# Attention scores: ScalarE casts half of the first two units, and the transposes of k or q of a unit share one PSUM tile of 8 KB per partition

## Chip, cores, metric

One core of one Trainium2 chip, one launch. The metric is device time in microseconds (us). Time before: 202.47 us, median of 3 runs (202.41 to 202.62).

## The reference

Scores of attention without softmax, for 8 batches x 8 heads x 512 positions x 64 dimensions, all in float32:

```python
def reference(q, k):
    scale = 1.0 / np.sqrt(q.shape[-1])
    return (np.einsum('bhqd,bhkd->bhqk', q, k) * scale).astype(np.float32)
```

It reads 16.78 MB and writes 67.11 MB, whatever the kernel does between.

## The kernel before

It works in four units of two batches. Per unit it loads k and q in float32 (4.19 MB), casts them to bf16, transposes them on TensorE through PSUM, copies the result to SBUF, and then makes four output tiles of 4.19 MB. An output tile takes eight evacuations, turn by turn on ScalarE and VectorE, and leaves with one store. Inputs and outputs share one pool of three buffers of 32 KB per partition. The copies of the next unit's transposes are put between the evacuations of the present unit by a generator, `ahead`. All DMAs are issued by SyncE (SP), on one queue.

```python
    W = 8                      # transposes per PSUM tile; JP = 16 per unit for k, 16 for q
    big_pool = ctx.enter_context(tc.tile_pool(name="big", bufs=3))
    tpsum_pool = ctx.enter_context(tc.tile_pool(name="tpsum", bufs=2, space=bass.MemoryType.PSUM))
    psum_pool = ctx.enter_context(tc.tile_pool(name="psum", bufs=2, space=bass.MemoryType.PSUM))
    # ... cut ...
    def load_and_cast(v):
        xf = big_pool.tile([P, 2, 2, J * D], f32, name="big")
        both = []
        for x, src in enumerate((k_r, q_r)):
            nc.sync.dma_start(out=xf[:, x], in_=src[v].rearrange("p (s c) -> p s c", s=2))
        for x in range(2):
            xb = bf_pool.tile([P, JP, 2, D, 2], bf16, name="xb")
            wide = (1, RO)[x]
            for s in range(2):
                pinned(nc.gpsimd.tensor_copy(out=..., in_=...))      # 128x2048
            both.append(words(xb.rearrange("p j s d e -> p j (s d e)")))
        return both

    def rearrange(tp, pattern, dst):
        nonlocal n_tp
        copy = (nc.vector.tensor_copy, nc.scalar.copy)[n_tp % 2]
        n_tp += 1
        for s in range(2):                       # two halves of the partitions
            src = tp[half(s)].rearrange(pattern, n=N, h=2)
            for h in range(2):
                pinned(copy(out=dst(s, h), in_=src[:, h]))
                yield
    # transpose(v, kb, qb): W transposes into one tp, then rearrange(tp), for k and then for q

    def scores(v, t):
        kT, qz = ts[v]
        o = big_pool.tile([P, 2, RO, S], f32, name="big")
        for x in range(2):
            n = 2 * t + x
            for i in range(0, RO, 2):
                ps = psum_pool.tile([P, 2, S], f32, name="ps")
                # ... two matmuls into ps ...
                evacuate(o[:, x, i:i + 2, :], ps)
                yield
        nc.sync.dma_start(out=out_r[v, t], in_=o.rearrange("p x i k -> p x (i k)"))
    # ... cut ...
    cast = [load_and_cast(v) for v in range(UNITS)]
    for _ in transpose(0, *cast[0]):
        pass
    for v in range(UNITS):
        ahead = transpose(v + 1, *cast[v + 1]) if v + 1 < UNITS else iter(())
        for t in range(TILES):
            for n, _ in enumerate(scores(v, t)):
                take(ahead, 1 if v == 0 else int(n in (0, 2, 3, 5, 6)))
```

`pinned` keeps each engine's order of work as the program has it; the framework adds the waits.

Of the kernel before, what the change touches and what calls it, by code (L numbers as in the profile page):

```python
# [1 line left out]

# [5 lines left out]


@with_exitstack  # L10
def kernel(
    ctx: ExitStack,
    tc: tile.TileContext,
    q: bass.AP,
    k: bass.AP,
    out: bass.AP,
):







    nc = tc.nc
    B, H, S, D = q.shape
    scale = 1.0 / (D ** 0.5)
    P = 128
    UNITS = B // 2
    N = H  # L30
    M = P // (2 * H)
    R = S // M
    J = R // 2
    RO = 8
    U = S // RO
    JP = J // 2
    JJ = J // RO // 2
    W = 8
    IW = W // JJ
    TILES = N // 2  # L40

    f32 = mybir.dt.float32
    bf16 = mybir.dt.bfloat16

    q_r = q.rearrange("(v b) g (m j) d -> v (b g m) (j d)", b=2, j=R)
    k_r = k.rearrange("(v b) g (m j) d -> v (b g m) (j d)", b=2, j=R)
    out_r = out.rearrange("(v b) (t x h) (u i) k -> v (b t) (h u) x (i k)", b=2, x=2, h=2, i=RO)

    consts = ctx.enter_context(tc.tile_pool(name="consts", bufs=1))

    big_pool = ctx.enter_context(tc.tile_pool(name="big", bufs=3))
    bf_pool = ctx.enter_context(tc.tile_pool(name="bf", bufs=6))
    t_pool = ctx.enter_context(tc.tile_pool(name="t", bufs=2))
    tpsum_pool = ctx.enter_context(tc.tile_pool(name="tpsum", bufs=2, space=bass.MemoryType.PSUM))
    psum_pool = ctx.enter_context(tc.tile_pool(name="psum", bufs=2, space=bass.MemoryType.PSUM))


    pinned = tc.keep_in_program_order

    n_evac = 0  # L60
    n_tp = 0

    def evacuate(dst, src):
        nonlocal n_evac
        if n_evac % 2 == 0:
            pinned(nc.scalar.mul(out=dst, in_=src, mul=scale))  # L66
        else:
            pinned(nc.vector.tensor_scalar(out=dst, in0=src, scalar1=scale, scalar2=None,  # L68
                                           op0=mybir.AluOpType.mult))
        n_evac += 1  # L70

    def half(h):
        return slice(h * D, (h + 1) * D)

    def words(ap):
        return ap.bitcast(f32)

    def load_and_cast(v):

        xf = big_pool.tile([P, 2, 2, J * D], f32, name="big")  # L80
        both = []
        for x, src in enumerate((k_r, q_r)):
            nc.sync.dma_start(out=xf[:, x], in_=src[v].rearrange("p (s c) -> p s c", s=2))
        for x in range(2):
            xb = bf_pool.tile([P, JP, 2, D, 2], bf16, name="xb")

            wide = (1, RO)[x]
            for s in range(2):
                pinned(nc.gpsimd.tensor_copy(  # L89
                    out=xb[:, :, s].rearrange("p (g i) d e -> p g e i d", i=wide),  # L90
                    in_=xf[:, x, s].rearrange("p (g e i d) -> p g e i d", e=2, i=wide, d=D)))
            both.append(words(xb.rearrange("p j s d e -> p j (s d e)")))
        return both

    def rearrange(tp, pattern, dst):

        nonlocal n_tp
        copy = (nc.vector.tensor_copy, nc.scalar.copy)[n_tp % 2]
        n_tp += 1
        for s in range(2):  # L100
            src = tp[half(s)].rearrange(pattern, n=N, h=2)
            for h in range(2):
                pinned(copy(out=dst(s, h), in_=src[:, h]))  # L103
                yield

    def transpose(v, kb, qb):


        kT = t_pool.tile([P, N, M, 2, J], bf16, name="kT")
        qz = qzs[v % 2]  # L110
        ts[v] = (kT, qz)
        kw = words(kT)
        qw = words(qz)
        for j0 in range(0, JP, W):
            tp = tpsum_pool.tile([P, W, P], f32, name="tp")
            for j in range(W):
                pinned(nc.tensor.transpose(out=tp[:, j, :], identity=identity, in_=kb[:, j0 + j]))  # L117
            yield
            yield from rearrange(tp, "d j (n h m) -> d h n m j",
                                 lambda s, h: kw[half(h), :, :, s, j0:j0 + W])  # L120
        for i0 in range(0, RO, IW):
            tp = tpsum_pool.tile([P, IW, JJ, P], f32, name="tp")
            for i in range(IW):
                for jj in range(JJ):
                    pinned(nc.tensor.transpose(out=tp[:, i, jj, :], identity=identity,  # L125
                                               in_=qb[:, RO * jj + i0 + i]))
            yield
            yield from rearrange(tp, "d i jj (n h m) -> d h i n m jj",
                                 lambda s, h: qw[half(h), i0:i0 + IW, :, h * U // 2:(h + 1) * U // 2]
                                 .rearrange("d i n (m s jj) -> d s i n m jj", s=2, jj=JJ)[:, s])  # L130
# [9 lines that stand above are left out]
                for w in range(2):  # L140
                    pinned(nc.tensor.matmul(out=ps[:, w, :], lhsT=qz[:, i + w, n, :],  # L141
                                            rhs=kT[:, n].rearrange("d m s j -> d (m s j)"),
                                            start=True, stop=True))
# [4 lines that stand above are left out]
    def take(steps, count):  # L148
        for _ in range(count):
            next(steps, None)  # L150

    identity = consts.tile([P, P], dtype=f32)
    make_identity(nc, identity)
    qzs = [consts.tile([P, RO, N, P], bf16, name=f"qz{n}") for n in range(2)]
    for qz in qzs:
        nc.vector.memset(qz, 0.0)  # L156
    cast = [load_and_cast(v) for v in range(UNITS)]

    ts = {}
    for _ in transpose(0, *cast[0]):  # L160
        pass
    for v in range(UNITS):
        ahead = transpose(v + 1, *cast[v + 1]) if v + 1 < UNITS else iter(())
        for t in range(TILES):
            for n, _ in enumerate(scores(v, t)):

                take(ahead, 1 if v == 0 else int(n in (0, 2, 3, 5, 6)))
        for _ in ahead:
            pass


# [1 line left out]
_INS = ['q', 'k']  # L173
_OUTS = [((8, 8, 512, 512), 'float32')]


# [23 lines left out]
```

## Time and profile before

| | before |
|---|---|
| time, span | 202.47 us, 200.7 us |
| DMA queue busy | 98.3% of the span |
| busiest compute engines | VectorE 53%, TensorE 52%, ScalarE 42% |
| first store issued; loads through | 36.81 us; about 41.7 us |
| smallest time from issue to landing of a store | 16.0 us |

The prediction below shows the lines. Read it with one thing in mind: when the DMA queue is full from 4 us to the end (a share of 1.01 and 430 GB/s from 4 to 190 us), an engine matters only through the moment at which its work lets the next DMA be issued.

Two more stretches of the kernel before serve for comparison later, the passage from loads to stores and the stores (length, busy time of PE, PEld, VectorE, ScalarE and GpSimd, granted clock, DMA share, GB/s):

```profile
41.00:44.00 3.00, 1.78 (x6) 0.57 (x6) 2.96 (x4) 1.64 (x3) 2.74 (x2) 1.00 0.93 393
44.00:190.00 146.00, 85.10 (x298) 32.80 (x297) 82.56 (x76) 69.19 (x77) 4.04 (x2) 0.82 1.01 430
```

### The profile page before, as it was taken

The numbers are of one execution on the slowest core, as the hardware profiler recorded it, in microseconds if no ns is written. First come the engines' busy times: TensorE is split into PE (matmuls) and PEld (weight loads), VectorE is DVE, ScalarE is ACT, GpSimd is POOL, SyncE is SP. The second block draws the span as 40 slices with busy tenths as digits, with TensorE's granted clock in tenths as the row PEclk, the third lists the DMA queues.
The fourth block names the chain that finished last, engine by engine and source line by source line (L and its number), as shares of the span: only waits on it lengthen the run. The fifth ranks groups of instructions, "written<-read, shape, count | busy, mean of one in ns | idle before, by whom it ended". The sixth has DMA issues, their size and how long they took to land.

```text
span 200.7 us, 1143 instructions
## 1 busy us (share of the span) xinstructions
PE 105.3 (52%) x384; PEld 45.8 (23%) x384; DVE 106.8 (53%) x98; ACT 85.0 (42%) x97; POOL 39.5 (20%) x22
## 2 busy tenths in 40 slices
PE   0035758566657465478637496748585667510000
PEld 0034535223214131224313122312121111100000
DVE  6705538486475976485749357844444444630000
ACT  2004423864755629253844384366435243620000
POOL 1299999995000000000000000000000000000000
PEclk9999576999699999957999759975858858975555
DMA  6999999999999999999999999999999999999994
GB/s 206 424 444 437 421 421 441 434 395 421 434 424 441 428 431 431 433 426 434 431 428 424 434 441 424 431 431 434 424 431 434 431 424 431 428 437 428 428 428 199
DMA packets 5509, 83.95 MB, mean 418 GB/s; under 512 B 384, under 2 KB 384, under 8 KB 384
## 3 DMA queue, kind: packets, MB, share of 16 engines
q1 hardware_dynamic: 5504, 83.89, 98.3%
q8 instruction: 3, 0.05, 0.1%
q14 instruction: 2, 0.02, 0.0%
HBM read 16.78 MB, written 67.11 MB: 418 GB/s over the span
## 4 chain that ended last, share of the span: by engine, by line
DMA 40%; DVE 10%; PE 8%; ACT 6%; issue 1%; ACTq 0%; SPq 0%; DVEq 0%
DMA out_dram<-big 40%; DVE big L68 9%; PE ps L141 8%; ACT big L66 5%; ACT qz L103 1%; DVE qz L103 1%; ACTq L66 0%; SPq L146 0%; DVEq L68 0%
## 5 line engine op out<-in xcount | busy, mean ns | idle before, releaser
L141 PE MATMUL ps<-kT,qz 128*128 128x512 bf16 x256 | 87.6, 447 | 55.5 <-ACT big L66 41.6
L68 DVE TENSOR_SCALAR big<-ps 128x1024 f32<-128x1024 f32 x64 | 78.4, 1224 | 59.8 <-PE ps L141 37.2
L66 ACT ACTIVATE big<-ps 128x1024 f32<-128x1024 f32 x64 | 65.5, 1023 | 73.0 <-PE ps L141 37.2
L141 PEld LDWEIGHTS <-qz 128*128 128x128 bf16 x256 | 27.2, 106 | 111.0 <-issue 97.5
L89 POOL CAST xb<-big 128x2048 bf16<-128x2048 f32 x16 | 38.8, 2468 | 7.9 <-DMA big<-in_k_dram 7.3
L117 PE MATMUL tp<-identity,xb 128*128 128x128 f32 x64 | 11.6, 346 | 13.4 <-POOL xb L89 13.4
L103 ACT COPY kT<-tp 64x512 f32<-64x512 f32 x16 | 9.2, 577 | 15.3 <-PE tp L117 15.1
L103 DVE COPY kT<-tp 64x512 f32<-64x512 f32 x16 | 11.0, 686 | 6.3 <-PE tp L117 6.0
L117 PEld LDWEIGHTS tp<-identity,xb 128*128 128x128 f32 x64 | 10.5, 184 | 15.2 <-POOL xb L89 13.4
L103 DVE COPY qz<-tp 64x512 f32<-64x512 f32 x16 | 11.0, 687 | 2.7 <-PE tp L125 2.5
L103 ACT COPY qz<-tp 64x512 f32<-64x512 f32 x16 | 9.6, 602 | 2.9 <-PE tp L125 2.7
L125 PE MATMUL tp<-identity,xb 128*128 128x128 f32 x64 | 9.4, 300 | 2.5 <-ACT kT L103 2.5
L125 PEld LDWEIGHTS tp<-identity,xb 128*128 128x128 f32 x64 | 8.5, 156 | 4.3 <-issue 3.3
L156 DVE MEMSET qz<- 128x4096 uint32 x2 | 6.9, 3472 | 2.5 <-PEq L184 1.7
L103 ACT ACT_TABLE_LOAD x1 | 1.3, 1283 | 0.7 <-PEq L184 0.7
masks.py:199 POOL TENSOR_SCALAR_AFFINE_SELECT identity<-identity 128x128 f32<-128x128 f32 x1 | 0.3, 292 | 0.1
masks.py:197 POOL MEMSET identity<- 128x128 f32 x1 | 0.2, 204 | 0.3 <-POOLq L184 0.3
L184 POOL MEMSET const-float32-0.0<- 128x1 f32 x1 | 0.1, 98 | 0.2 <-issue 0.2
L184 POOL MEMSET const-bfloat16-1.0<- 128x1 bf16 x1 | 0.1, 101 | 0.0
L184 POOL MEMSET const-uint8-127<- 128x1 uint8 x1 | 0.1, 101 | 0.0
L184 POOL MEMSET const-float32-1.0<- 128x1 f32 x1 | 0.1, 98 | 0.0
## 6 DMA issues: line engine op xcount, KB each, us to landing
out_dram<-big SPq DMA_DIRECT2D x16, 4096.0 KB, 20.7
big<-in_k_dram SPq DMA_DIRECT2D x4, 2048.0 KB, 18.1
big<-in_q_dram SPq DMA_DIRECT2D x4, 2048.0 KB, 22.7
```

The source lines that it names most:

```text
L66: pinned(nc.scalar.mul(out=dst, in_=src, mul=scale))
L68: pinned(nc.vector.tensor_scalar(out=dst, in0=src, scalar1=scale, scalar2=None, op0=mybir.AluOpType.mult))
L89: pinned(nc.gpsimd.tensor_copy(out=xb[:, :, s].rearrange("p (g i) d e -> p g e i d", i=wide), in_=xf[:, x, s].rearrange("p (g e i d) -> p ...
L103: pinned(copy(out=dst(s, h), in_=src[:, h]))
L117: pinned(nc.tensor.transpose(out=tp[:, j, :], identity=identity, in_=kb[:, j0 + j]))
L125: pinned(nc.tensor.transpose(out=tp[:, i, jj, :], identity=identity, in_=qb[:, RO * jj + i0 + i]))
L141: pinned(nc.tensor.matmul(out=ps[:, w, :], lhsT=qz[:, i + w, n, :], rhs=kT[:, n].rearrange("d m s j -> d (m s j)"), start=True, stop=True))
L156: nc.vector.memset(qz, 0.0)
L184: nc = _bacc.Bacc("TRN2", target_bir_lowering=False, num_devices=1)
```

## The change

The intent is to start sooner and to copy in larger pieces: ScalarE takes half of the casts of units 0 and 1, so that a load is cast in half the time; 16 transposes go into one PSUM tile of 8 KB per partition (16 x 128 float32; before, two tiles of half that), which leaves in four wide copies instead of eight; and for unit 0, whose copies nothing else covers, the two engines take turns at these copies.

```diff
-    W = 8
+    W = 16
-    tpsum_pool = ctx.enter_context(tc.tile_pool(name="tpsum", bufs=2, space=bass.MemoryType.PSUM))
+    tpsum_pool = ctx.enter_context(tc.tile_pool(name="tpsum", bufs=1, space=bass.MemoryType.PSUM))
@@ load_and_cast(v) becomes load(v), which issues the two loads, and cast(v, xf)
-                pinned(nc.gpsimd.tensor_copy(
+                to_bf16 = nc.scalar.copy if s and v < 2 else nc.gpsimd.tensor_copy
+                pinned(to_bf16(
@@ rearrange
-        copy = (nc.vector.tensor_copy, nc.scalar.copy)[n_tp % 2]
+        copies = (nc.vector.tensor_copy, nc.scalar.copy)
+        first = len(ts) == 1
         n_tp += 1
-                pinned(copy(out=dst(s, h), in_=src[:, h]))
+                pinned(copies[(n_tp + h * first) % 2](out=dst(s, h), in_=src[:, h]))
@@ body
-    cast = [load_and_cast(v) for v in range(UNITS)]
+    xfs = [load(v) for v in range(3)]
     ts = {}
-    for _ in transpose(0, *cast[0]):
+    for _ in transpose(0, *cast(0, xfs[0])):
         pass
+    xfs.append(load(3))
+    casts = [None] + [cast(v, xfs[v]) for v in range(1, UNITS)]
-                take(ahead, 1 if v == 0 else int(n in (0, 2, 3, 5, 6)))
+                take(ahead, int(n in ((1, 3, 6), (1, 4))[t % 2]))
```

More of the change, by code (lines that the diff above doesn't have):

```diff
@@ L76, in words, with load, cast @@
         return ap.bitcast(f32)
-    def load_and_cast(v):
+    def load(v):
         xf = big_pool.tile([P, 2, 2, J * D], f32, name="big")
-        both = []
         for x, src in enumerate((k_r, q_r)):
             nc.sync.dma_start(out=xf[:, x], in_=src[v].rearrange("p (s c) -> p s c", s=2))
+        return xf
+    def cast(v, xf):
+        both = []
         for x in range(2):
@@ L156 @@
         nc.vector.memset(qz, 0.0)
-    cast = [load_and_cast(v) for v in range(UNITS)]
+    xfs = [load(v) for v in range(3)]
     ts = {}
-    for _ in transpose(0, *cast[0]):
+    for _ in transpose(0, *cast(0, xfs[0])):
         pass
+    xfs.append(load(3))
+    casts = [None] + [cast(v, xfs[v]) for v in range(1, UNITS)]
     for v in range(UNITS):
-        ahead = transpose(v + 1, *cast[v + 1]) if v + 1 < UNITS else iter(())
+        ahead = transpose(v + 1, *casts[v + 1]) if v + 1 < UNITS else iter(())
         for t in range(TILES):
             for n, _ in enumerate(scores(v, t)):
-                take(ahead, 1 if v == 0 else int(n in (0, 2, 3, 5, 6)))
+                take(ahead, int(n in ((1, 3, 6), (1, 4))[t % 2]))
         for _ in ahead:
```

## The prediction

> **What bounds the kernel now.** I read the page first, then windows of the DMA share, then the waits of the DMA queue, then the order of time in the first 60 us, because the change works mostly there.
>
> The page, DMA queue and traffic (packets, MB, share of the span of 16 engines):
>
> ```profile
> q1 hardware_dynamic: 5504, 83.89, 98.3%
> HBM read 16.78 MB, written 67.11 MB: 418 GB/s over the span
> ```
>
> Every byte crosses one queue, and that queue is busy for 98.3% of the span. No compute engine passes 53%. The stretches (columns: length, busy PE, PEld, DVE, ACT, POOL, clock, DMA share, GB/s) show where the other 1.7% lies:
>
> ```profile
> 0.00:2.00 2.00, 0.00 (x0) 0.00 (x0) 0.34 (x1) 1.26 (x1) 0.70 (x6) 1.00 0.42 82
> 2.00:4.00 2.00, 0.00 (x0) 0.00 (x0) 2.00 (x1) 0.02 (x1) 0.00 (x0) 1.00 0.65 221
> 4.00:31.00 27.00, 10.96 (x49) 8.26 (x50) 12.94 (x14) 6.83 (x10) 22.20 (x10) 0.87 1.01 433
> 41.00:43.00 2.00, 1.20 (x5) 0.40 (x5) 1.99 (x3) 1.25 (x2) 1.92 (x1) 1.00 0.89 369
> 4.00:190.00 186.00, 105.29 (x384) 45.83 (x384) 104.45 (x98) 83.73 (x96) 38.80 (x16) 0.83 1.01 430
> ```
>
> A ramp in the first 4 us moves 2 x 82 + 2 x 221 = 606 KB; then it is flat at 430 GB/s. The rest, 83.28 MB at 430 GB/s, takes 193.7 us, so the stream ends near 198 us, and some 2.5 us of tail give the span of 200.7. The time reported, 202.47, is 1.8 us above the span. The only dip is at 41 to 43 us: 2 us x (430 - 369) / 430 = 0.3 us. It lies where the loads end and the stores begin: summing the stretches, the 16.78 MB of loads are through at about 41.7 us.
>
> So the question for any change is: **does each store stand in the queue before the queue runs dry?** A store has 4.19 MB, 9.75 us at 430 GB/s. The stores by line (count, ns, first and last start; then issue to landing):
>
> ```profile
> L146 SPq DMA_DIRECT2D out_dram<-big x16: 372/372/403, 36.8 to 178.1; - x16
> DMA to landing us min/median/max: 16.0/20.7/22.0
> ```
>
> 9.75 us of transfer and about 2 us of completion (the tail again, an estimate) leave at least 16.0 - 11.8 = 4.3 us of standing in the queue for the tightest store, and 20.7 - 11.8 = 9 us for the median one. The queue is therefore never short of work. The issues at the start are at 36.81, 47.49, 56.55 and 64.24 us; they are needed at 41.7, 51.7, 61.4 and 71.2 (one transfer after another). The slacks are 4.9, 4.2, 4.9 and 7.0 us. These are what the change may spend for nothing, or gain for nothing.
>
> The opening, in order of time (start, length):
>
> ```profile
> 8.58 34.34 POOL L89 CAST xb<-big 128x2048 bf16<-128x2048 f32 x14 [7.28 <-DMA big<-in_k_dram]
> 13.44 3.68 PE L117 MATMUL tp<-identity,xb 128*128 128x128 f32 x16 [13.44 <-POOL xb L89]
> 19.61 2.57 PE L125 MATMUL tp<-identity,xb 128*128 128x128 f32 x16 [2.49 <-ACT kT L103]
> 23.57 1.03 PE L141 MATMUL ps<-kT,qz 128*128 128x512 bf16 x2 [1.40 <-DVE qz L103]
> 28.13 1.02 ACT L66 ACTIVATE big<-ps 128x1024 f32<-128x1024 f32 x1 [3.42 <-POOL xb L89]
> 36.81 0.40 SPq L146 DMA_DIRECT2D out_dram<-big  x1
> ```
>
> GpSimd casts without a pause, and the first output tile waits for it: that tile takes the buffer of unit 1's input, free only when unit 1 is cast. Later tiles wait for a landed store:
>
> ```profile
> SPq L146 <- DVE big L68: 152.5, 16, 17.6
> ACT big L66 <- DMA out_dram<-big: 31.3, 12, 3.5
> DVE big L68 <- DMA out_dram<-big: 15.5, 9, 2.5
> ```
>
> The queue's 152.5 us of waiting for VectorE looks like a bound by VectorE; it isn't, because stores already issued keep running during it.
>
> [...]
>
> **The change part by part.** Rows used (busy us, mean ns):
>
> ```profile
> L68 DVE TENSOR_SCALAR big<-ps 128x1024 f32<-128x1024 f32 x64 | 78.4, 1224 | 59.8 <-PE ps L141 37.2
> L66 ACT ACTIVATE big<-ps 128x1024 f32<-128x1024 f32 x64 | 65.5, 1023 | 73.0 <-PE ps L141 37.2
> L89 POOL CAST xb<-big 128x2048 bf16<-128x2048 f32 x16 | 38.8, 2468 | 7.9 <-DMA big<-in_k_dram 7.3
> L103 ACT COPY kT<-tp 64x512 f32<-64x512 f32 x16 | 9.2, 577 | 15.3 <-PE tp L117 15.1
> L103 DVE COPY kT<-tp 64x512 f32<-64x512 f32 x16 | 11.0, 686 | 6.3 <-PE tp L117 6.0
> ```
>
> *Casts.* Four of GpSimd's 16 casts go to ScalarE. GpSimd loses 4 x 2.47 = 9.9 us. ScalarE gains 4 casts of 2048 elements; from 577 ns at 512 and 1023 at 1024 the slope is 0.87 ns per element, so about 1.9 us each, 7.6 us in all. Beside each other, half a load is cast in 2.5 us instead of 4.9.
>
> *Copies.* 64 copies of 512 elements become 32 of 1024. Taking the evacuations as a measure (1.22 and 1.02 us), a unit's copies cost VectorE 4 x 1.22 = 4.9 us instead of 8 x 0.687 = 5.5, and ScalarE 4.1 instead of 4.7. That saves 0.6 us per unit and engine, 2.4 us per engine in all, none of it on the DMA path.
>
> *Buffers.* The four PSUM banks were two tiles and become one. The transposes of q can no longer run during the copies of k, and sixteen transposes come in one burst (16 x 0.30 to 0.35 = 5 us of TensorE).
>
> *The opening.* Loads land at 8.6, 13.4, then every 4.84 us: 18.3, 23.1, 27.9, 32.8, 37.6, 43. k of unit 0 is cast at 11.1 (was 13.4) and transposed at 14.8 (16 in 3.68 us). ScalarE must first cast its half of q (13.4 to 15.3). Four copies follow. If the two engines exclude each other[...], they take 3.5 us[...] to 4.6 us, ending at 18.9 to 20.0. q is transposed in 2.6 us, 21.5 to 22.6, and copied by 25.0 to 27.2. ScalarE next has unit 1's two casts, in program order before any evacuation: 3.8 us, so the first evacuation starts at 28.8 to 31.0, against 28.13. If the copies did overlap fully, it would be some 2 us before 28.13. The first tile took 36.8 - 28.1 = 8.7 us; with the burst I allow 9.3. **The first store is then issued at about 38.1 to 40.3** (35 if the copies overlap); it is needed at 41.7. The second tile needs the buffer of unit 2, whose halves GpSimd still casts alone: q lands at 32.8, two casts end at 37.7, as good as the 37.95 of before. Its 8 to 9 us end at 47 to 50, needed at 51.7. The third tile waits for unit 3, whose q lands at 43 with or without the change, cast at 48.0; with the burst of q's transposes ahead it ends near 57, needed at 61.4.
>
> *Later.* A tile with a burst takes some 11 us instead of 9, the next one 8, against 9.75 of transfer and 9 us of standing queue. Nothing runs dry.
>
> *Sum:* removed from the DMA path, 0; added, 0 to 1 us at the first store; bytes, rate, ramp and tail unchanged. 202.47 + 0.1 = 202.6 us.
>
> **The rivals.** (1) The earlier casts show at the end: if stores waited for compute in the opening, a start 2 us earlier would give 200.5 us. Against it: the queue still has 4.9 us of loads in it when the first store is issued. (2) The serial copies and the two extra ScalarE casts ahead of the first evacuation make the first store late. [...]the store comes at 42 to 43: the queue runs dry by about 1 us, 203.5. Against it: my worst sum without throttle is still 1.4 us early. (3) The single tile starves later stores: a tile would have to last over 19 us, or several in a row over 9.75; 206 or more. Against it: VectorE's sum is 24.5 us of 39 per unit, TensorE's 105.3 / 4 = 26.
>
> **Range and chances.** The three runs of before span 0.2 us[...]: floor 202.1. Rival 2, at one in five, sets the top: 203.8. Over 2% slower means 206.5, a hole of 4 us in the queue, of which I see no source: 0.02. Over 2% faster means 198.4, less than the stream's 193.7 us with its ramp, tail and the 1.8 us outside: 0.01.
>
> **What would show it right or wrong.** Right: queue share still 98%, 430 GB/s in the middle, first store between 35 and 41 us, ScalarE's casts near 1.9 us, copies near 1.0 and 1.2 us, load of unit 3 issued near 16 us (was 18.3), the shortest store landing still over 12 us. The copies of unit 0 alternating without overlap confirm the exclusion. Wrong: a hole in the DMA row at 41 to 45 us or at any later store, or a rate other than 430 GB/s with the same bytes.

The forecast came to 202.6 us (202.47 + 0.1) with a range of 202.1 to 203.8. What is cut is what no trace or run shows: a section on the hardware; the reason why two engines should exclude each other on PSUM; in rival 2, the 1 to 2 us by which a lower granted clock was to lengthen the transposes, on which its 42 to 43 us rested in part; and 0.3 us for another chip, which puts the floor below the runs. That the engines exclude each other stands as a supposition, and its 3.5 to 4.6 us as estimate from the evacuations: 3.5 is 1.22 + 1.22 + 1.02, two of the four copies side by side, and 4.6 is some 2 x (1.22 + 1.02), all in a row. "Banks" is a name for parts of the PSUM tile: all four are the changed kernel's whole tile.

## The result, and the profile after

204.05 us, median of 4 runs (203.7 to 204.36), against 202.48 us (202.41 to 202.62) for the kernel before on the same chip: ratio 1.0076, 95% interval 1.0058 to 1.0094. Here and below a ratio is the mean time of one kernel's fast runs over that of the other's fast runs of the same rounds, so it isn't quite the ratio of the medians. The change costs 0.8%: within 2%, as the prediction said, but above its range, whose top was 203.8.

The page of the changed kernel, queue and traffic:

```profile
q1 hardware_dynamic: 5504, 83.89, 98.1%
HBM read 16.78 MB, written 67.11 MB: 415 GB/s over the span
```

Packets and bytes are the same, and the queue's busy share hardly moved. But 98.1% of 202.2 us is 198.3 us of busy time, against 98.3% of 200.7, 197.3 us. **The same packets took 1.0 us longer.** The stretches of the changed kernel show where:

```profile
41.00:44.00 3.00, 1.78 (x6) 0.57 (x6) 1.58 (x3) 2.93 (x4) 2.96 (x2) 1.00 0.89 377
44.00:190.00 146.00, 84.00 (x306) 34.90 (x311) 86.08 (x71) 68.26 (x68) 3.67 (x2) 0.86 1.01 426
```

At 41 to 44 us it moved 377 GB/s instead of 393, a loss of 3 us x 16 / 430 = 0.1 us. In the 146 us of stores after it, the rate is 426 instead of 430, with no stretch of the share below full. That is the surprise: 1% less rate for the rest of the run, in a stretch in which nothing waits for compute.

The opening of the changed kernel in order of time (start, length):

```profile
11.05 3.65 PE L124 MATMUL tp<-identity,xb 128*128 128x128 f32 x16 [11.05 <-POOL xb L94]
13.33 2.46 ACT L94 CAST xb<-big 128x2048 bf16<-128x2048 f32 x1 [2.43 <-DMA big<-in_q_dram]
...
15.66 0.99 ACT L110 COPY kT<-tp 64x1024 f32<-64x1024 f32 x1
...
16.69 1.22 DVE L110 COPY kT<-tp 64x1024 f32<-64x1024 f32 x1 [7.28 <-ACT kT L110]
17.94 1.01 ACT L110 COPY kT<-tp 64x1024 f32<-64x1024 f32 x1 [1.29 <-DVE kT L110]
...
20.36 3.65 PE L132 MATMUL tp<-identity,xb 128*128 128x128 f32 x16 [5.66 <-DVE kT L110]
...
28.65 4.83 ACT L94 CAST xb<-big 128x2048 bf16<-128x2048 f32 x2
...
33.56 1.02 ACT L66 ACTIVATE big<-ps 128x1024 f32<-128x1024 f32 x1
33.57 1.22 DVE L68 TENSOR_SCALAR big<-ps 128x1024 f32<-128x1024 f32 x1 [6.01 <-ACT xb L94]
...
41.15 0.40 SPq L153 DMA_DIRECT2D out_dram<-big  x1
```

The casts are earlier, as intended: k of unit 0 reaches TensorE at 11.05 us instead of 13.44. Then the gain is given back. The two engines' copies stand one behind the other, each released by the other engine; q's transposes wait for the last of them; and the casts of unit 1 keep ScalarE from 28.65 to 33.5 us, so the first evacuation comes at 33.56 instead of 28.13 us. VectorE, which has no cast of its own to do, waits for these casts too, 6.01 us: the first output tile takes the buffer of unit 1's input, which is free only when unit 1 is cast. The first store is issued at 41.15 instead of 36.81. It finds the queue at its end. The changed kernel's stores, issue to landing:

```profile
DMA to landing us min/median/max: 11.9/19.8/22.6
```

The smallest value, 11.9 against 16.0 before, is that of this first store (landed near 53.1 us): 9.75 us of it are the transfer of 4.19 MB at 430 GB/s, which leaves hardly any standing in the queue.

For the sizes, the trace also has each DMA packet's start, duration and bytes, though not its engine; sums are divided by 16. Worked out from those records: the 16 DMA engines were without a packet for 0.24 us on average between 40.5 and 45 us (before: 0), and the 16 KB packets took 198.31 us per engine in all instead of 197.25. Span after less span before is 202.18 - 200.74 = 1.44 us. **An empty time of 0.24 and longer packets of 1.06 make 1.30 of it**; the rest is in the ends. Before, 95% of the packets from 44 to 90 us took 611 or 612 ns; after, 23%, and their mean was 617.8 instead of 611.6.

So there are two things to explain: why the first store is late, and why a store late by so little slows the packets until the end.

### The profile page after: what moved, and what is told of

Same layout as the page of the kernel before. It is cut to its first block, busy times and chain, and to the rows that moved or that the text cites. A ratio compares the mean times of both kernels' runs of the same rounds, so it can differ in the third digit from the quotient of the medians.

```text
span 202.2 us, 1105 instructions
## 1 busy us (share of the span) xinstructions
PE 102.6 (51%) x377; PEld 47.3 (23%) x384; DVE 104.3 (52%) x82; ACT 91.8 (45%) x85; POOL 29.9 (15%) x18
## 3 DMA queue, kind: packets, MB, share of 16 engines
q1 hardware_dynamic: 5504, 83.89, 98.1%
## 4 chain that ended last, share of the span: by engine, by line
DMA 39%; DVE 13%; PE 11%; ACT 7%; issue 1%; another core or an unknown queue 0%; ACTq 0%; DVEq 0%; SPq 0%
DMA out_dram<-big 39%; DVE big L68 11%; PE ps L148 9%; ACT big L66 6%; DVE qz L110 2%; ACT kT L110 1%; PE tp L124 1%; PE tp L132 1%; ACTq L66 0%; DVEq L68 0%; SPq L153 0%
## 5 line engine op out<-in xcount | busy, mean ns | idle before, releaser
L148 PE MATMUL ps<-kT,qz 128*128 128x512 bf16 x249 | 81.9, 430 | 59.1 <-ACT big L66 38.4
L148 PEld LDWEIGHTS <-qz 128*128 128x128 bf16 x256 | 26.5, 104 | 111.0 <-issue 92.0
L94 POOL CAST xb<-big 128x2048 bf16<-128x2048 f32 x12 | 29.2, 2464 | 17.1 <-DMA big<-in_k_dram 12.1
L110 DVE COPY qz<-tp 64x1024 f32<-64x1024 f32 x14 | 17.1, 1221 | 5.2 <-PE tp L132 3.8
L124 PE MATMUL tp<-identity,xb 128*128 128x128 f32 x64 | 13.1, 390 | 11.7 <-POOL xb L94 11.0
L124 PEld LDWEIGHTS tp<-identity,xb 128*128 128x128 f32 x64 | 12.2, 211 | 13.5 <-POOL xb L94 11.0
L110 ACT COPY kT<-tp 64x1024 f32<-64x1024 f32 x14 | 14.0, 1002 | 1.5 <-DVE kT L110 1.3
L94 ACT CAST xb<-big 128x2048 bf16<-128x2048 f32 x4 | 9.8, 2472 | 8.9 <-DMA big<-in_k_dram 6.4
L132 PE MATMUL tp<-identity,xb 128*128 128x128 f32 x64 | 9.4, 310 | 5.7 <-DVE kT L110 5.7
L132 PEld LDWEIGHTS tp<-identity,xb 128*128 128x128 f32 x64 | 8.7, 162 | 6.6 <-issue 6.0
L110 DVE COPY kT<-tp 64x1024 f32<-64x1024 f32 x2 | 2.4, 1223 | 8.4 <-ACT kT L110 8.4
L110 ACT COPY qz<-tp 64x1024 f32<-64x1024 f32 x2 | 2.0, 1019 | 7.6 <-DVE qz L110 7.6
```

Source lines behind the costliest of these rows:

```text
L94: pinned(to_bf16(out=xb[:, :, s].rearrange("p (g i) d e -> p g e i d", i=wide), in_=xf[:, x, s].rearrange("p (g e i d) -> p g e i d", e=2, ...
L110: pinned(copies[(n_tp + h * first) % 2](out=dst(s, h), in_=src[:, h]))
L124: pinned(nc.tensor.transpose(out=tp[:, j, :], identity=identity, in_=kb[:, j0 + j]))
L132: pinned(nc.tensor.transpose(out=tp[:, i, jj, :], identity=identity, in_=qb[:, RO * jj + i0 + i]))
L148: pinned(nc.tensor.matmul(out=ps[:, w, :], lhsT=qz[:, i + w, n, :], rhs=kT[:, n].rearrange("d m s j -> d (m s j)"), start=True, stop=True))
```

## Experiments

Theory A: the queue running dry once is the cause of both losses; after the restart the packets are longer. Theory B: the changed steady state (wide copies, one PSUM tile) slows the stores. All runs gave correct results. The packet figures are from the trace's packet records, packets over 700 ns left out; "empty" is the mean time without a packet at 40.5 to 45 us.

### 1. The changed kernel without turns in unit 0

```diff
-                pinned(copies[(n_tp + h * first) % 2](out=dst(s, h), in_=src[:, h]))
+                pinned(copies[n_tp % 2](out=dst(s, h), in_=src[:, h]))
```

> The changed kernel without the alternation of the two engines in unit 0: k of unit 0 is copied by ScalarE alone, q by VectorE alone. ScalarE is then free for unit 1's casts while VectorE copies q, so the first evacuation should start at about 28.5 us and the first store be issued near 36 us instead of 41.15. Theory A (the queue ran dry once at 41 to 43 us, and the restart leaves the 16 DMA engines in step, so that packets take 617 ns instead of 611): no hole, packets back at 611 to 612 ns, 202.5 us. Theory B (the changed steady state, wide copies and one PSUM tile, slows the stores): still 204 us, packets near 617 ns.

Measured: 202.92 us (202.38 to 203.03), ratio 1.0012 (1.0 to 1.0023). The first store in its issue order:

```profile
40.21 0.40 SPq L153 DMA_DIRECT2D out_dram<-big  x1
```

It came later than I expected (36), since the first tile took over 10 us, but 0.9 us sooner than in the changed kernel, and the queue was never empty. Packets were at 612.2 ns to 90 us, then 615.1 and 616.4. Taking away one part, which has nothing to do with the steady state, gives back 1.1 of 1.6 us. The six runs fall into two groups: 202.38 and 202.40, as fast as the kernel before, and four of 202.87 to 203.03; the trace is of the slower group. That the packets lengthen late even so wasn't expected.

### 2. The changed kernel with unit 1 cast by GpSimd

```diff
-                to_bf16 = nc.scalar.copy if s and v < 2 else nc.gpsimd.tensor_copy
+                to_bf16 = nc.scalar.copy if s and v < 1 else nc.gpsimd.tensor_copy
```

> The changed kernel with ScalarE casting for unit 0 only; unit 1 is cast by GpSimd alone, as before the change. The alternation in unit 0 stays. Unit 1 is cast at 28.1 us by GpSimd (two casts after q lands at 23.2), so the first evacuation starts near 29 us instead of 33.6 and the first store is issued near 36.5 us. Theory A: no hole, 202.5 us, packets 611 to 612 ns. Theory B: 204 us, packets near 617 ns.

Measured: 202.71 us (202.52 to 203.23), ratio 1.0013 (1.0 to 1.0026). First evacuation at 29.86, first store at 39.20 us (36.5 was expected), no empty time, packets at 611.7 ns to 90 us, though 615.7 from 125 us on. Either part alone, taken away, removes most of the loss: the turns and the casts of unit 1 on ScalarE are late only together.

### 3. The kernel before with a late first store

```diff
+                if (v, t, n, i) == (0, 0, 1, RO - 2):
+                    for _ in range(9):
+                        pinned(nc.vector.memset(idle, 0.0))      # idle: [128, 512] f32
                 evacuate(o[:, x, i:i + 2, :], ps)
```

> The kernel before, with nine memsets of a scratch tile (some 0.49 us each, 4.4 us) put on VectorE ahead of the last evacuation of the first tile, so that the first store is issued at about 41.2 us as in the changed kernel; nothing else differs. Theory A: a hole of some 0.25 us at 41 to 43 us, then packets near 617 ns to the end, 203.7 to 204.3 us. Theory B: only the hole's own 0.25 us, 202.7 us.

Measured: 204.86 us (204.54 to 204.89), ratio 1.0111 (1.0098 to 1.0124), above the expected 203.7 to 204.3, for the first store came at 41.84 us instead of 41.2. A memset took 0.48 us, as expected, but 0.17 us of waiting stood between two of them. Its passage from loads to stores, and its stores:

```profile
41.00:44.00 3.00, 2.19 (x9) 1.70 (x9) 1.89 (x2) 1.03 (x1) 2.97 (x2) 0.50 0.68 289
44.00:190.00 146.00, 85.06 (x303) 34.90 (x307) 85.58 (x79) 70.66 (x78) 3.98 (x2) 0.84 1.00 426
```

The rate of the stores is the changed kernel's 426, not the kernel before's 430, although every cast, copy and PSUM tile is the kernel before's. The sum closes: 0.95 us empty at the first store, 0.26 at the second, which also came late, and 198.36 - 197.25 = 1.11 us of longer packets make 2.32; the span grew by 203.1 - 200.7 = 2.4.

### 4. The changed kernel with its first tile stored in two halves

```diff
                 evacuate(o[:, x, i:i + 2, :], ps)
+                if (v, t) == (0, 0) and i == RO - 2:
+                    nc.sync.dma_start(out=out_r[v, t][:, x], in_=o[:, x].rearrange("p i k -> p (i k)"))
                 yield
-        nc.sync.dma_start(out=out_r[v, t], in_=o.rearrange("p x i k -> p x (i k)"))
+        if (v, t) != (0, 0):
+            nc.sync.dma_start(out=out_r[v, t], in_=o.rearrange("p x i k -> p x (i k)"))
```

> The changed kernel with its first output tile stored in two halves, the first after four of the eight evacuations, so that it stands in the queue near 37.5 us, before the loads are through at 41.7 us. Theory A: no hole, 202.5 us with packets at 611 to 612 ns, though every copy, cast and PSUM tile is the changed kernel's. Theory B: 204 us.

Measured: 202.93 us (202.51 to 202.99), ratio 1.0015 (1.0003 to 1.0027). The first half is issued at 37.59 us; no empty time; packets at 611.7 ns to 90 us and 613.6 in the last third. All of the changed kernel's computing is left as it was, and most of the loss is gone. Theory B falls as an account of the loss; why 0.15% is left isn't shown.

### 5. The kernel before, first store less late

```diff
-                    for _ in range(9):
+                    for _ in range(5):
```

> The kernel before with five memsets on VectorE ahead of the last evacuation of the first tile instead of nine (nine moved the first store from 36.81 to 41.84 us, 0.56 us each), so the first store comes at about 39.6 us, still ahead of the end of the loads at 41.7. A control for the memsets. Theory A (only an empty queue counts): no hole, 202.5 us, most store packets at 611 ns to the end. Rival C (any delay of the first store, or the memsets' own writes, costs time in proportion): 2.34 us for nine memsets gives 1.3 us for five, 203.8 us.

Measured: 202.67 us (202.43 to 202.83), ratio 1.0004 (0.9992 to 1.0016); first store at 38.84 us, 2.0 us later than in the kernel before, and free. The loss isn't in proportion to the delay; rival C falls. The packets weren't quite what theory A expected: they lengthened late, to 614.5 ns from 125 us on.

### 6. The kernel before with a late ninth store

As experiment 3, with 17 memsets in unit 2, first tile.

> The kernel before with seventeen memsets on VectorE ahead of the last evacuation of the ninth tile (third unit, first tile), so that the ninth store is issued at about 120.2 us instead of 110.74; the queue of stores runs dry at about 119.9 us less the start of a store, so a hole of some 1 us opens near 120 us. Theory A: packets near 611.5 ns before the hole and near 617 ns after it, to the end; the loss is the hole and 5 ns x 124 packets per engine = 0.6 us, 204.0 to 204.2 us. If the slow packets were something of the opening (loads beside stores, casts beside stores), packets stay at 611.5 ns after this hole and the time is 203.5 us.

Measured: 206.21 us (205.62 to 206.63), ratio 1.0178 (1.0162 to 1.0195). The ninth store came at 122.53 us, later than planned, so the empty time was larger. The stretches around it:

```profile
44.00:118.00 74.00, 42.01 (x173) 18.48 (x176) 51.49 (x57) 37.48 (x42) 3.81 (x2) 0.90 1.01 430
118.00:124.00 6.00, 1.36 (x3) 0.35 (x3) 4.78 (x7) 0.43 (x1) 0.00 (x0) 0.50 0.41 175
124.00:190.00 66.00, 32.92 (x120) 12.37 (x120) 35.73 (x31) 31.69 (x35) 0.00 (x0) 0.89 1.01 428
```

By the packet records, packets took 611.5 ns at 100 to 118 us and 618.6 at 124 to 145 us; 96% of them had 611 or 612 ns before the empty time and 21% after. The span grew by 4.0 us: 3.27 empty, 197.97 - 197.25 = 0.72 longer packets. **After an early and after a late empty time, the slow packets begin there and stay to the end.** They belong to no stage of the kernel.

### 7. and 8. Each half of the change alone

The casts alone (transposes, PSUM tiles and copies as before; ScalarE casts half of units 0 and 1):

```diff
-    W = 16
+    W = 8
-    ... name="tpsum", bufs=1 ...
+    ... name="tpsum", bufs=2 ...
-                pinned(copies[(n_tp + h * first) % 2](...))
+                pinned(copies[(n_tp + 1) % 2](...))
-                take(ahead, int(n in ((1, 3, 6), (1, 4))[t % 2]))
+                take(ahead, 1 if v == 0 else int(n in (0, 2, 3, 5, 6)))
```

> The casts of the change alone: ScalarE casts half of units 0 and 1 in the changed kernel's order of work, but transposes, PSUM tiles, copies and their places are those of the kernel before. I expect unit 1 cast at about 27.5 us, the first store near 36 us, no hole and 202.5 us. If ScalarE's 2.47 us casts alone make the first store late, 204 us.

Measured: 202.58 us (202.42 to 202.59), ratio 0.9999 (0.9986 to 1.0012). First store at 38.15 us (36 was expected), packets at 611.6 ns.

The PSUM tile and the copies alone (all casts on GpSimd):

```diff
-                to_bf16 = nc.scalar.copy if s and v < 2 else nc.gpsimd.tensor_copy
+                to_bf16 = nc.gpsimd.tensor_copy
```

> The other part alone: one four-bank PSUM tile, wide copies, alternation in unit 0 as in the changed kernel, but all casts on GpSimd. k of unit 0 is cast at 13.4 us, transposed at 17.1, copied at 21.7, q transposed at 25.3 and copied at 29.9; first evacuation near 31 us, first store near 40 us. Theory A: just ahead of the hole, 202.5 to 203.0 us; above 40.8 us a hole opens and the time is 203.7 or more. Theory B (wide copies slow the stores) was already refuted by the two stores in halves, and expects 204 us here too.

Measured: 203.43 us (203.05 to 203.84), ratio 1.0042 (1.003 to 1.0053), slower than expected for a first store at 40.54 us. The engines were without a packet for 0.01 us only, yet the packets were at 614.7 ns from 44 to 90 us and at 617.0 after: 0.9 us in all, which is the whole loss. So theory A is too narrow. The queue needn't be empty: a store that joined within about half a microsecond of the end of the loads was enough here (40.54 us against the 40.9 to 41.0 that are worked out below).

### 9. Copies of unit 0 split by halves of the PSUM tile

```diff
-                pinned(copies[(n_tp + h * first) % 2](out=dst(s, h), in_=src[:, h]))
+                if first:                        # g = 0: the tile's first eight transposes, g = 1: its last eight
+                    for g in range(2):
+                        pinned(copies[g](out=dst(s, h)[part], in_=src[:, h][part]))   # part: half g of j, or of i
+                else:
+                    pinned(copies[n_tp % 2](out=dst(s, h), in_=src[:, h]))
```

> The changed kernel with the copies of unit 0 split between the engines by PSUM bank instead of by half: VectorE copies what lies in the tile's first two banks, ScalarE what lies in the last two, 64x512 each. [...]the two now run beside each other, and each tile of unit 0 is emptied in about 2.8 us instead of 4.55; with VectorE starting after the first eight transposes the first store is issued at about 37 us instead of 41.15, no hole, 202.5 to 202.7 us. If the engines exclude each other by the whole tile, nothing moves: 204 us or more, for 16 copies in series take about 5 us for each tile.

Measured: 204.5 us (204.41 to 204.95), ratio 1.0095 (1.008 to 1.011): the second branch. (The first takes the waiting to go by the part of the tile that is read; its 2.8 us is an estimate, four copies of 0.69 us.) The copies of k in order of time:

```profile
15.79 0.57 ACT L117 COPY kT<-tp 64x512 f32<-64x512 f32 x1
...
16.39 0.68 DVE L117 COPY kT<-tp 64x512 f32<-64x512 f32 x1 [0.85 <-ACT kT L117]
17.11 0.58 ACT L117 COPY kT<-tp 64x512 f32<-64x512 f32 x1 [0.75 <-DVE kT L117]
17.71 0.69 DVE L117 COPY kT<-tp 64x512 f32<-64x512 f32 x1 [0.64 <-ACT kT L117]
```

They wait for each other (0.64 to 0.85 us) even where they read different halves of the tile. The tile that they write, `kT`, is not the reason: in the kernel before, both engines wrote into the same `kT` at once, from two PSUM tiles, 17.15 to 18.24 us:

```profile
15.45 2.79 DVE L103 COPY kT<-tp 64x512 f32<-64x512 f32 x4 [6.04 <-PE tp L117]
17.15 2.35 ACT L103 COPY kT<-tp 64x512 f32<-64x512 f32 x4 [15.13 <-PE tp L117]
```

In these programs the two engines exclude each other on a whole PSUM tile, by waits on each other's semaphores (the releasers in the lines above); taking turns within one tile gained nothing. The first store came at 41.70 us, with 0.71 us empty and 1.28 us of longer packets, 1.99 in all, for a span 2.0 us longer.

### 10. to 13. Why are the packets longer?

A suspicion: after a common restart the 16 DMA engines begin their packets together and hinder each other. As a measure of "in step" I take the starts of the packets of a stretch as angles on a circle of 611 ns and average them: 0 is evenly spread, 1 is all at once. At 44 to 54 us it is 0.13 before, 0.85 after and 0.86 with the copies split by halves of the tile (bank_split).

I tried to take the engines out of step behind the first store of the changed kernel, with small loads meant to use unequal numbers of engines, and equal ones in the control. Whether they did, the trace can't show, for it doesn't name a packet's engine; what the expectations said of the share of each engine, and of the time of the small loads, was the author's estimate, shown by no trace, and is cut:

```diff
         nc.sync.dma_start(out=out_r[v, t], in_=o.rearrange("p x i k -> p x (i k)"))
+        if (v, t) == (0, 0):
+            for g, rows in enumerate(range(15, 0, -1)):    # control: [16] * 8
+                nc.sync.dma_start(out=spare[:rows, g], in_=k_r[0][:rows, :256])
```

> The changed kernel, with fifteen loads of 1 KB rows into a scratch tile nobody reads, queued right behind the first store: one of 15 rows, one of 14, and so on to 1 row. [...] The hole at 41 to 43 us stays. Theory A1 (the packets are slow because the engines run in step): packets near 617 ns during the first store, near 611.5 ns after the small loads at about 52 us; the time falls by up to 1.0 us[...], so 203.3 to 203.9 us. Rival A2 (after a hole packets are slow for another reason than their phase): 617 ns to the end, 204.5 us or more.

> The control for the staggered loads: eight loads of 16 rows of 1 KB in their place, about as many small packets in all[...]. Theory A1: packets stay near 617 ns to the end, 204.3 to 204.6 us. If small packets alone restore 611.5 ns, the phase is not shown by the staggered run.

Measured: 209.2 and 207.38 us, ratios 1.0321 and 1.0236. Both missed their purpose. The issuing queue stopped at the eighth small load until the first store had landed near 53 us. That is a wait of the program. In the trace of the changed kernel the 24 DMAs land on eight semaphores in turn, three each; counted on in the same way, the eighth small load takes the first store's once more, and the staggered run's trace has the wait:

```profile
SPq L156 <- DMA out_dram<-big: 3.8, 1, 3.8
```

So the second store was issued at 55.77 and 53.36 us, after new and larger empty times. They only repeat the finding: packets of 617 to 620 ns behind those.

With fewer, larger pieces (rows of 704 floats; 14, 11, 8, 6 and 3 rows, and 16, 16 and 16 rows for the control) the queue didn't stall, and the second store came at 48.45 and 48.64 us:

> The staggered loads once more, few enough not to stall the issuing queue (it stalled at the eighth small load): five loads of 14, 11, 8, 6 and 3 rows of 2.8 KB behind the first store of the changed kernel[...]. Theory A1 (slow because in step): packets near 617 ns until about 52 us, near 611.5 to 613 ns afterwards, 203.4 to 204.0 us. A2 (slow for another reason): 617 ns to the end, 204.3 us or more.

> The control: three loads of 16 rows of 2.8 KB[...]. A1: packets near 617 ns to the end, 204.3 to 204.5 us. If this too goes back to 611.5 ns, the phase is not what matters.

Measured: 204.5 us (ratio 1.0104, 1.0089 to 1.0118) and 204.3 us (1.0088, 1.0074 to 1.0103). Behind the small loads at 52 us:

```text
                 in step            mean packet, ns (packets over 700 ns left out)
run              44-54   60-70 us   43-51   55-65   65-90   100-118   124-145 us
before           0.13    0.08       611.3   611.7   611.6   611.5     611.5
changed          0.85    0.85       620.6   617.4   618.1   616.4     616.3
stagger5         0.37    0.45       617.8   612.2   614.8   615.0     615.1
no_stagger3      0.60    0.29       618.9   611.4   611.7   614.2     616.2
```

In both runs the packets went from about 618 ns back to about 612 at the small loads, so the slow state can be left again. But the control did it better than the staggered run, and the prediction for it was wrong: three equal small loads took the engines further out of step (0.29) than unequal ones (0.45), perhaps through the passage between loads and stores, which I hadn't thought of; that isn't shown. Both kernels paid for it at that passage and won no time.

### Nine kernels by the time of the first store

```text
run                 first store  empty   mean packet, ns          in step  median time
                    us           us      44-90  90-125  125-190   44-54    us
before              36.81        0       611.6  611.6   612.2     0.13     202.48
casts_alone         38.15        0       611.6  611.6   612.5     0.17     202.58
before_delay_5      38.84        0       611.7  612.5   614.5     0.37     202.67
unit1_on_gpsimd     39.20        0       611.7  611.9   615.7     0.34     202.71
one_engine_copies   40.21        0       612.2  615.1   616.4     0.16     202.92
psum_alone          40.54        0.01    614.7  617.0   616.4     0.41     203.43
changed             41.15        0.24    617.8  616.8   616.4     0.85     204.05
bank_split          41.70        0.71    618.0  616.8   616.4     0.86     204.5
before_delay_9      41.84        0.95    617.8  616.5   616.7     0.66     204.86
```

**The order by first store is the order by time**, across two quite different kernels. Left out are the kernels that store or load otherwise: the late ninth store, the small loads, and the two halves, which with 37.59 us and 202.93 us would not fit the order. Up to about 39 us a delay is free or nearly so; from 40 us on, the packets pass into a slow state (616 to 618 ns) sooner and sooner; from 41 us on, the empty time is added. The empty times of the last three give the deadline itself: 41.15 - 0.24, 41.70 - 0.71 and 41.84 - 0.95 are all 40.9 to 41.0 us.

What stays open is why the packets get longer. The in-step measure, taken over stretches of 2.5 us, goes with it in many places: without turns it rose from 0.14 at 75 to 85 us to 0.60 at 105 to 115 us, while the packets went from 612.8 to 615.2 ns. But not everywhere: with five memsets it was 0.08 at 165 to 175 us, and the packets had 614.9 ns. Nor does it always take a late store: the kernel before, too, comes to 613.9 ns at 175 to 185 us. Only one trace per kernel was read for this. No kernel here beat the kernel before; the casts alone equal it.

## Why the prediction was wrong, point by point

- **The bound** was right: the queue is the limit, and the change touches the time only where a store is late.
- **The failing step is the sum's "bytes, rate, ramp and tail unchanged".** The rate did not stay: 430 became 426 GB/s over 146 us. The range took a late store to cost its own empty time and nothing else. It cost 0.24 us of that and 1.06 us of longer packets. Experiments 3, 4 and 6 show that this follows a late store and not the copies.
- **Rival 2 is what happened**: the first store late through serial copies and two more casts on ScalarE. It put the empty time at 1 us and gave it one chance in five. It should have been the main line.
- **The first store**, 38.1 to 40.3 us predicted, was issued at 41.15. Against the late end of each term: ScalarE's cast, 1.9 us from the slope of the copies, took 2.47, which puts the two casts of unit 1 at 4.8 us instead of 3.8. The transposes of q, 2.6 us, took 3.65. The 2.6 came from one trace; in the three traces of the kernel before with memsets, which come only later, they took 3.04, 3.49 and 3.65. Together with the copies of k and q, this made the first evacuation some 2.5 us later than the late end of the forecast. The first tile then took 41.15 - 33.56 = 7.6 us instead of 9.3, for most of TensorE's burst of transposes (31.22 to 34.87 us) ran while ScalarE was still casting. The burst was put at 5 us, a sum of mean durations that overlap; it took 3.65, as the prediction's own line of 16 in 3.68 us says.
- **A lower granted clock**, to which rival 2 gave 1 to 2 us, isn't shown as the cause: the granted clock was 0.50 here (20.3 to 24.1 us), but without turns the same 16 transposes took 3.65 us at a granted 1.00, as did those of k at 11.05 us.
- **The deadline**, 41.7 us, was really 40.9: it left out the time from issue to first packet, which was 0.89 us for the late store of experiment 6 (issued at 122.53, first packet at 123.42 us).
- **The exclusion on PSUM** was right in its effect: the four copies of k took 15.66 to 20.21 us, 4.55, where I gave 3.5 to 4.6. The reason given for it was shown by no trace; in these programs the exclusion is by tile (experiment 9).
- **Copies** (1.00 and 1.22 us), the load of unit 3 (issued at 15.86 us; 16 predicted), the second store (48.84 us; 47 to 50) and the third (58.10; near 57) were as predicted. The bursts starved no later store, so rival 3 is out; rival 1, a gain from the earlier casts, did not show either.

## What to carry to other kernels

Where one queue bounds a kernel, find for each store the latest moment at which it may be issued, and keep a margin of a few microseconds there: in these runs 2 us of margin cost nothing that shows (before_delay_5, ratio 1.0004), while one under one microsecond already cost up to 0.4% with next to no gap (0.01 us), because the packets after it took longer (psum_alone, 614.7 to 617.0 ns instead of 611.6). Before giving an engine more work early on, list what stands behind that work in its program order, and which buffers wait for it; casts shared out so that each load is done sooner can still make the first store later (41.15 us instead of 36.81, with the turns at the copies; 38.15 with the casts alone). And in these programs two engines that take turns within one PSUM tile don't run beside each other (four copies of k in 4.55 us); give each its own tile, as in the kernel before, where the copies of k ran beside each other from 17.15 to 18.24 us.
